# First value tiles in float32 from raw rows, and a new order at the head of a hybrid decoder step

## The chip, the cores and the metric

The kernel runs on one core of a Trainium2 chip. The metric is device time in microseconds (us) for one execution, the median of three runs. Five engines work side by side, each through its own queue in order: TensorE (PE, matmuls), VectorE (DVE), ScalarE (ACT), GpSimd (POOL) and SyncE (SP), whose queue issues the DMAs. Operands lie in SBUF, matmul results in PSUM, and inputs, outputs and scratch in HBM.

## The reference, cut to what matters

One inference step of a one-layer decoder, for a prompt of 2048 rows and for a decode batch of 64 rows (called the sample), with 1024 columns.

```python
h = rmsnorm(x, norm_w)                      # per row, then a weight for each column
z = h @ w_in                                # (2048 + 64) x 1024 by 1024 x 3600
q, k, v, qb, kb, vb, g_lr, gate_a, gate_b = jnp.split(z, split_points(), axis=-1)
q = rope(rmsnorm(heads(q, H_A), q_norm_w), pos)
k = rope(rmsnorm(heads(k, H_A), k_norm_w), pos)
o_a = attend(q, k, v)                       # three dilated windows, mixed by softmax weights
o_b, s_fin = gla_chunked(...)               # gated linear attention
y = x + (concat(o_a * silu(gate_a), rmsnorm(o_b) * silu(gate_b)) @ w_out)
```

The change touches the first 512 rows of the norm and of the products q, k and v.

## The kernel before, in words

The prompt is 16 tiles of 128 rows; the contraction over 1024 columns is 8 blocks (KT) of 128. Float32 accuracy comes from float16 pairs: rows and weights are each split into a high and a low part, and `project` adds three float16 products for each block (high by high, high by low, low by high), so one tile of one 512-wide output is 24 matmuls of 128x512 into a PSUM tile `acc_v_<tile>`, `acc_q_<tile>` and so on (pool `ps_Y`, two buffers).

Rows. `fetch` loads a tile of x. `squares` sums the squares of its rows (ScalarE, result `jk` thrown away), `rsqrt` makes the row factor `rs` on VectorE and ScalarE. For the first four tiles `prep_first` makes the high part on ScalarE and the low part on VectorE (`parts_of_rows`, tile `early_ht`), turns both by 16 float16 transposes on TensorE (`turned`, PSUM tiles `th_<tile>_<part>`), copies the turned high part by ScalarE and the low part by VectorE to `hl_<tile>`, and stores `hl` to `h_d` for later blocks. The sample's rows are normed (`x_s`), turned by 8 float32 transposes (`ptx`) and split to `hs`.

Weights. `fetch_w` loads 8 raw blocks of 128x512 (`wr_v`, `wr_q`, `wr_k`). `load_w` bounds them: for v, q and k VectorE takes the largest magnitude of each row of each block (`wm`), for the other blocks ScalarE sums squares (`jw`). `spread_max` takes the largest over the partitions by a transpose and a one-column matmul on TensorE (`mx`), with a VectorE reduction between the two. From it comes a power of two (`pw`), then the factors `ns`, and then each raw block gives a high part on ScalarE and a low part on VectorE (tile `w_v`, `w_q`, `w_k`).

Results. `post` handles a finished tile: for v ScalarE scales it to `vs` (stored as output) and makes `vp` (with VectorE's low part), which frees the PSUM tile. For q and k ScalarE makes the squares `sq` and the copy `zs`, then POOL and VectorE do the norm and the rotation, and ScalarE and VectorE write the parts `qp` or `kp`.

At the head (`first(0)`) v is computed for the sample and tiles 0 to 3, then q and k for tiles 0 to 3. After that come the other tiles with attention mixed in, the remaining projections, the linear attention and the output projection.

The order of each engine's queue is not the order of the code. `ORDER` lists, engine by engine, numbers of instructions in the order in which the code issued them; `in_order` binds the scheduler to that list. The lists come from a planner and are fixed for a kernel, so a change in what is issued comes with lists of its own for the whole kernel.

Of the kernel before, what the change touches and what calls it, by code (L numbers as in the profile page):

```python
# [18 lines left out]
P = 128  # L19
# [728 lines left out]
def tile_hymba(ctx: ExitStack, tc: tile.TileContext, A: dict):  # L748
# [276 lines left out]
    with ExitStack() as c1:  # L1025
# [153 lines left out]
        def prep_first(w_v):  # L1179
# [47 lines left out]
            for a in range(2):  # L1227
                turned(0, a)
# [1367 lines left out]
```

## Time and profile before

| | |
|---|---|
| runs | 1200.03, 1197.94, 1202.1 us; median 1200.03 |
| the profiled execution | 1201.56 us, its span on the core 1199.8 us |
| busy: TensorE / VectorE / ScalarE / POOL | 1162.0 / 919.0 / 785.1 / 542.2 us |
| TensorE idle, whole span | 37.8 us |
| TensorE busy in the first 40 us | 22.84 us |
| mean granted TensorE clock | 0.996 |
| moved by DMA | 283.13 MB, mean 236 GB/s |

A row of the instructions in order of time gives start and duration in us, engine, line, operation, output <- inputs, shapes and count; rows of equal instructions that follow each other are merged, and the bracket tells how long the engine was idle before it and what ended that. A row's duration of a matmul runs from its issue to the end of its way through the array, so that it overlaps the next one's.

### The profile page before, as it was taken

How to read it: one execution, taken by the hardware profiler on the slowest of the kernel's cores; microseconds unless marked ns; L12 is line 12 of the kernel's file. 1: busy time of each engine (PE TensorE's matmuls, PEld its weight loads, DVE VectorE, ACT ScalarE, POOL GpSimd, SP SyncE). 2: the span in 40 equal slices, each digit the busy share in tenths (PEclk: the TensorE clock that was granted, in tenths of full speed). 3: DMA queues.
4: the chain of work that ended last, by engine and by line, in shares of the span. 5: the costliest groups of instructions: out<-in, count | busy, mean ns of one | idle time of the engine just before them, and what ended most of it. 6: DMA issues, size and time to landing. Idle time of an engine off the chain costs nothing.

```text
span 1199.8 us, 27149 instructions
## 1 busy us (share of the span) xinstructions
PE 1162.0 (97%) x9542; PEld 714.5 (60%) x9542; DVE 919.0 (77%) x2489; ACT 785.1 (65%) x2152; POOL 542.2 (45%) x478
## 2 busy tenths in 40 slices
PE   4999999999999899999999999999999999999998
PEld 2544575566666566766777766646656566655543
DVE  7887888898989958878777755689788989743642
ACT  6645698778679968878767643777798764422220
POOL 0054444665548344662454558664534544311310
PEclk9999999999999999999999999999999999999999
DMA  8578967889768898799999977856672477999962
GB/s 292 196 188 203 252 186 145 228 216 233 165 196 227 199 254 282 245 279 273 281 267 256 278 225 212 256 181 232 205 258 85 137 263 263 320 392 398 375 216 79
DMA packets 235834, 283.13 MB, mean 236 GB/s; under 512 B 116193, under 2 KB 146866, under 8 KB 232626
## 3 DMA queue, kind: packets, MB, share of 16 engines
q1 hardware_dynamic: 235698, 281.40, 78.3%
q8 instruction: 75, 1.23, 0.4%
q14 instruction: 61, 0.50, 0.1%
HBM read 183.02 MB, written 75.24 MB: 215 GB/s over the span
## 4 chain that ended last, share of the span: by engine, by line
PE 81%; DVE 9%; ACT 3%; issue 3%; DMA 1%; POOL 1%; SPq 0%; POOLq 0%; DVEq 0%; ACTq 0%
PE Y L2181 12%; PE acc_q L1822 7%; PE acc_k L1822 7%; PE acc_qkb L1822 7%; PE acc_v L1822 6%; PE acc_vb L1822 6%; PE acc_g L1822 6%; PE t L1105 5%; PE s L1087 5%; PE acc_gb L1822 4%; PE O L1120 4%; PE OS L2438 2%; PE sc_e L932 1%; DVE p L1095 1%; PE tm L2146 1%
## 5 line engine op out<-in xcount | busy, mean ns | idle before, releaser
L1677 POOL TENSOR_TENSOR pr<-k,qb 128x512 f32<-128x512 f32 x128 | 168.8, 1319 | 126.6 <-DVE sck L1678 108.8
L1822 PEld LDWEIGHTS <-hr 128*128 128x128 f16 x1824 | 165.8, 98 | 86.9 <-issue 7.3
L1120 PE MATMUL O<-v,pt 128*128 128x64 f16 x1800 | 212.3, 193 | 3.6 <-POOL pt L1072 1.1
L1098 ACT ACTIVATE p<-p,st 128x256 f32<-128x256 f32 (+1 forms) x384 | 173.3, 454 | 36.0 <-DVE st L1095 35.0
L2181 PE MATMUL Y<-w_o,mh 128*128 128x512 f16 x768 | 187.4, 380 | 0.3 <-DVE xr L2188 0.3
L1120 PEld LDWEIGHTS <-pt 128*128 128x128 f16 x1800 | 145.5, 100 | 60.9 <-ACT pt L1064 2.7
L1822 PEld LDWEIGHTS <-hl 128*128 128x128 f16 x1248 | 116.8, 99 | 95.3 <-issue 1.8
L1072 POOL TENSOR_TENSOR pt<-p,pt 128x512 f16<-128x512 f32 (+1 forms) x80 | 95.6, 1195 | 151.4 <-DVE pt L1071 67.1
L1105 PE MATMUL t<-ident,p 128*128 128x128 f32 x600 | 147.5, 287 | 2.2 <-DVE pt L1065 1.2
L1822 PE MATMUL acc_g<-w_g,hr 128*128 128x272 f16 (+1 forms) x768 | 127.6, 276 | 0.9 <-ACT vbs L1460 0.9
L1087 PE MATMUL s<-kk,qq 128*128 128x256 f16 (+1 forms) x512 | 113.3, 265 | 1.2 <-DVE st L1095 0.9
L1822 PE MATMUL acc_v<-w_v,hl 128*128 128x512 f16 x384 | 113.5, 383 | 0.3 <-ACT hl L1195 0.3
L1822 PE MATMUL acc_vb<-w_vb,hr 128*128 128x512 f16 x384 | 113.3, 379 | 0.0
L1822 PE MATMUL acc_q<-w_q,hl 128*128 128x512 f16 x384 | 112.5, 379 | 0.0
L2181 PEld LDWEIGHTS <-mh 128*128 128x128 f16 x768 | 70.7, 98 | 68.5 <-issue 4.0
L1822 PE MATMUL acc_k<-w_k,hl 128*128 128x512 f16 x384 | 109.6, 379 | 0.2 <-DVE vp L1473 0.2
L1095 DVE CUSTOM_DVE_ANT_0 p<-s,m3w,scl_s 128x128 f32<-128x128 f32 (+1 forms) x256 | 92.7, 394 | 20.3 <-PE s L1087 9.0
L1678 DVE TENSOR_REDUCE sck<-pr 128x8 f32<-128x512 f32 x128 | 86.9, 679 | 23.5 <-POOL pr L1677 23.3
L1822 PE MATMUL acc_gb<-w_gb,hr 128*128 128x512 f16 x384 | 98.4, 380 | 0.8 <-DVE so_gb L1357 0.8
L1105 PEld LDWEIGHTS t<-ident,p 128*128 128x128 f32 x600 | 80.4, 141 | 24.8 <-ACT p L1098 3.8
L1822 PE MATMUL acc_qkb<-w_qkb,hr 128*128 128x512 f16 x288 | 85.9, 379 | 0.0
L1098 ACT ACTIVATION_READ_ACCUMULATOR p<-p,st 128x1 f32 x384 | 73.2, 191 | 0.0
(543 smaller groups left out, 2454.9 us busy)
## 6 DMA issues: line engine op xcount, KB each, us to landing
k<-in_cache_k_win SPq DMA_DIRECT2D x104, 256.0 KB
sv_b<-in_cache_v_win SPq DMA_DIRECT2D x24, 1024.0 KB
hr<-h_d SPq DMA_DIRECT2D x44, 512.0 KB
qb<-q_d SPq DMA_DIRECT2D x64, 256.0 KB
oc<-o_d SPq DMA_DIRECT2D x48, 264.0 KB
o_d<-o SPq DMA_DIRECT2D x64, 132.0 KB
x<-in_x_prompt SPq DMA_DIRECT2D x16, 512.0 KB
h_d<-hl SPq DMA_DIRECT2D x16, 512.0 KB
```

Of the source, the lines that this page charges most:

```text
L932: PE.matmul(sc[k0 : k0 + 64, o : o + 64], k[:, p * n + c * C + k0 : p * n + c * C + k0 + 64], qbd[:, :, p * (n // 2) + (c * C + k0) // 2 : ...
L1072: POOL.tensor_tensor(l, f, h, ALU.subtract)
L1087: PE.matmul(s_ps[:, i * w : (i + 1) * w], q, k, start=(n == 0), stop=(n == len(prods) - 1),)
L1095: DVE.tensor_tensor_reduce(s[:, sl], s_ps[:, sl], mask, neg, BIG, ALU.add, ALU.min, nmf(i))
L1098: ACT.activation(s[:, sl], s[:, sl], AF.Exp, bias=nmf(i), scale=-1.0, accum_out=denf(i))
L1105: PE.transpose(p_ps[:, i * P : (i + 1) * P], t["s"][:, i * P : (i + 1) * P], ident[:])
L1120: PE.matmul(o_, t["pt"][:, c, (i * nb + b) * P : (i * nb + b + 1) * P], vf(i, b)[:, d : d + HD], start=(b + n == 0), stop=(b == nb - 1 and ...
L1677: POOL.tensor_tensor(pr[:], kt, qt, ALU.mult)
L1678: DVE.tensor_reduce(out, pr[:].rearrange("p (u k d) -> p u k d", u=2, k=4), AX.X, ALU.add)
L1822: PE.matmul(z, a_[:, k, :], w[:, p_, k, cols], start=(k == 0 and i == 0), stop=(k == KT - 1 and i == 2),)
L2181: PE.matmul(Y[:], a_[:, k, :], w_[:, part, k, :512], start=(i == 0), stop=(i == len(prods) - 1),)
L2438: PE.matmul(OS[32 * x : 32 * x + 32, 0:256], ps(x), vs_[bb][:, 256 * u : 256 * u + 256], start=(i == 0), stop=(i == 13),)
```

## The change

1. `prep_first` multiplies tiles 0 and 1 by the raw weights of v in float32: raw rows `x` are turned by 8 float32 transposes for each tile (`xtp`), VectorE multiplies the turned rows by the norm weight while it takes them out of PSUM (`xt`, buffers `z4` and `z3`), and 8 float32 matmuls of 128x512 for each tile go straight to `acc_vx`. The row factor is applied when the result is taken out (`sc_v`, `exact_v`), so these two tiles of v need neither the split weights nor the split rows. They need both later, for q and k.
2. The row factors, parts and transposes come in the order tiles 2, 3, 0, 1. The sample's rows are loaded (`fetch("s")`, buffer `z3`, which tile 1's turned rows use first) and prepared behind all four tiles, and their product of v comes after the tiles'.
3. The bounds of w_q and w_k are made by sums of squares on ScalarE (`jw`), as those of the later weights are; w_v keeps the largest magnitudes.
4. Ten matmuls of a zero tile (`still` into `idle`) are issued ahead of all others.
5. The first DMAs are tile 0, the identity, one block of w_v, the norm weight, tile 1, the other blocks of w_v.

```diff
         def prep_first(w_v):
...
-            squares("s", ss[:NS, 0:1])
-            rsqrt(xp, rs[:NS, 0:1], ss[:NS, 0:1], 1.0 / D, NS, 1, "xs")
+            raws = fetched["v"]
+            zx = []
+            still = zp.tile([P, D], F16, name="still", tag="z1")
+            DVE.memset(still[:], 0.0)
+            idle = ps_O.tile([P, 512], F32, name="idle", tag="O")
+            for _ in range(10):
+                PE.matmul(idle[:], still[:, 0:P], still[:, 0:512], start=True, stop=True)
+            for t in range(2):
+                xt = zp.tile([P, KT, P], F32, name=f"xt_{t}", tag=("z4", "z3")[t], bufs=1)
+                for half in range(2):
...
+                    for i in range(4):
+                        k = 4 * half + i
+                        PE.transpose(pt[:, i], xs[t][:, k * P : (k + 1) * P], ident[:])
+                    DVE.tensor_tensor(
+                        xt[:, k4], pt[:], nw[:, k4].unsqueeze(2).to_broadcast([P, 4, P]), ALU.mult
+                    )
+                z = ps_Y.tile([P, 512], F32, name=f"acc_vx_{t}", tag="Y")
+                for k in range(KT):
+                    PE.matmul(z[:], xt[:, k], raws[k], start=(k == 0), stop=(k == KT - 1))
+                zx.append(z)
             squares(0, ss[:, 1:2])
             rsqrt(xp, rs[:, 1:2], ss[:, 1:2], 1.0 / D, P, 1, "x0", H_SCALE)
...
+            for t in range(2):
+                exact_v[t] = zx[t][:], sc[:, 0, t : t + 1], sc[:, 1, t : t + 1]
+            for t in (2, 3):
+                parts_of_rows(xs.pop(t), rs[:, t + 1 : t + 2], early_ht[:, t])
...
+            parts_of_rows(xs.pop(1), rs[:, 2:3], early_ht[:, 1])
+            for t in (2, 3, 0, 1):
+                for a in range(2):
+                    turned(t, a)
...
+            fetch("s")
+            squares("s", ss[:NS, 0:1])
...
-            exact = name in "vqk"
+            exact = name == "v"
...
-                ACT.activation(h, src, AF.Copy, scale=V_SCALE)
-                DVE.scalar_tensor_tensor(l, src, V_SCALE, h, ALU.mult, ALU.subtract)
+                by = exact_v[t][2] if t in exact_v else V_SCALE
+                ACT.activation(h, src, AF.Copy, scale=by)
+                DVE.scalar_tensor_tensor(l, src, by, h, ALU.mult, ALU.subtract)
...
-        fetch("s")
-        fetch_w("v", [0])
-        for t in (1, 2, 3):
+        fetch(0)
+        fetch_w("v", [1])
+        for t in (2, 3):
             fetch(t)
...
             for t in tiles:
+                if name == "v" and t in exact_v:
+                    z, by, _ = exact_v[t]
+                    post(name, z, by, P, t)
+                    yield
+                    continue
...
-                    for t in (["s"] if name == "v" else []) + tiles:
+                    for t in tiles + (["s"] if name == "v" else []):
```

`ORDER` is another list throughout; two of its lines:

```diff
-        "6-10 0 2 11 1 3-5 12-15 18 16 19-21 17 22-23 74 24-25 90-92 75 93 76 94-99 77 100-103 "
...
+        "0-7 10 14-17 11 8 12 26 13 30 27 31 28-29 32-33 18 34 19-23 42-43 35-41 44-45 24 46-48 "
...
```

TensorE's queue at the start of the program, before. `ptx` are the sample's transposes, `th` those of tile 0, `mx_v` the bound of w_v.

```order
L1219 MATMUL ptx_258<-ident,x_s 128x64 x4
L1189 LDWEIGHTS early_ht
L1189 MATMUL th_0_267<-ident_83,early_ht 128x128
L1257 MATMUL mx_v<-ident,w_v 1x128
L1219 MATMUL ptx_251<-ident,x_s 128x64
L1189 LDWEIGHTS early_ht
L1189 MATMUL th_0_267<-ident_83,early_ht 128x128
L1260 MATMUL mx_v<-mm_v,one_row 128x1
L1219 MATMUL ptx_251<-ident,x_s 128x64 x3
```

The same queue after, from the last of tile 1's float32 transposes (`xtp_..228` and `234`; those of tile 0, `206` and `212`, and eight of the zero matmuls stand ahead). `acc_vx_218` is tile 0's product, `acc_vx_240` tile 1's.

```order
L1217 MATMUL xtp_0_228<-ident,x_152 128x128 x2
L1217 MATMUL xtp_1_234<-ident,x_152 128x128 x2
L1223 MATMUL acc_vx_218<-wr_v_154,xt_205 128x512
L1223 MATMUL acc_vx_240<-wr_v_154,xt_227 128x512
L1223 MATMUL acc_vx_218<-wr_v_154,xt_205 128x512
L1223 MATMUL acc_vx_218<-wr_v_157,xt_205 128x512 x2
L1223 MATMUL acc_vx_218<-wr_v_161,xt_205 128x512 x2
L1292 MATMUL mx_v<-ident,w_v 1x128
L1295 MATMUL mx_v<-mm_v,one_row 128x1
L1223 MATMUL acc_vx_240<-wr_v_154,xt_227 128x512
```

Where the sample's and tile 0's transposes stood around the bound of w_v, there are now seven float32 products ahead of it, and nine behind it; all of tile 1's transposes stand ahead of the first product.

ScalarE's queue before, from the copy of the turned high part of tile 1 (`hl_191`) to the first parts of w_q.

```order
L1195 ACTIVATE hl_191<-th_0_319 128x1024
L1464 ACTIVATE vs_s<-za_446,wi_v 64x512
L1464 ACTIVATE vs_478<-acc_v_453,wi_v 128x512
L1472 ACTIVATE vp_481<-acc_v_453 128x8x64
L1195 ACTIVATE hl_192<-th_0_339 128x1024
L1195 ACTIVATE hl_193<-th_0_359 128x1024
L1338 ACTIVATE w_q<-wr_q_172,ns_q 128x512
L1338 ACTIVATE w_q<-wr_q_180,ns_q 128x512
```

The same queue after, from the fourth square of w_q's bound to the copy of the turned high part of tile 3 (`hl_191` is tile 3 here) and the root in w_q's bound.

```order
L1342 ACTIVATE jw_q_510,wm_q<-wr_q_176,nw 128x512
L1342 ACTIVATE jw_q_512,wm_q<-wr_q_178,nw 128x512
L1342 ACTIVATE jw_q_514,wm_q<-wr_q_180,nw 128x512
L1342 ACTIVATE jw_q_516,wm_q<-wr_q_182,nw 128x512
L1342 ACTIVATE jw_q_518,wm_q<-wr_q_184,nw 128x512
L1509 ACTIVATE vp_499<-acc_vx_240,sc_v 128x8x64
L1246 ACTIVATE early_ht<-x_152 128x1024
L1199 ACTIVATE hl_191<-th_0_350 128x1024
L1500 ACTIVATE vs_580<-acc_v_555,wi_v 128x512
L1355 ACTIVATE pw_q<-pw_q 128x1
L1273 ACTIVATE hs<-ptx_429 128x4x64
L1356 ACTIVATE pw_q<-pw_q 128x1
```

The squares of w_q, tile 1's `vp` and tile 0's high part now stand ahead of the copy that tile 3's product of v needs, and two more steps of the bound (`pw_q`) behind it.

More of the change, by code (lines that the diff above doesn't have):

```diff
@@ L1179, in prep_first @@
         def prep_first(w_v):
-            ss = xp.tile([P, 5], F32, name="ss_5", tag="ss5", bufs=1)
-            rs = xp.tile([P, 5], F32, name="rs_5", tag="rs5", bufs=1)
+            ss = xp.tile([P, 5], F32, name="ss_f", tag="ss5", bufs=1)
+            rs = xp.tile([P, 5], F32, name="rs_f", tag="rs5", bufs=1)
             hls = [hp.tile([P, 2, KT, P], F16, name=f"hl_{t}", tag="hl") for t in range(4)]
@@ L1195, in turned @@
                     ACT.activation(hls[t][:, a], pt[:], AF.Copy)
-            squares("s", ss[:NS, 0:1])
-            rsqrt(xp, rs[:NS, 0:1], ss[:NS, 0:1], 1.0 / D, NS, 1, "xs")
+            raws = fetched["v"]
[8 more added lines that the diff above has]
+                for half in range(2):
+                    pt = (ps_P, ps_S)[t].tile(
+                        [P, 4, P], F32, name=f"xtp_{t}_{half}", tag=("PT", "S")[t]
+                    )
+                    k4 = slice(4 * half, 4 * half + 4)
+                    for i in range(4):
[3 more added lines that the diff above has]
+                        xt[:, k4], pt[:], nw[:, k4].unsqueeze(2).to_broadcast([P, 4, P]), ALU.mult
+                    )
+                z = ps_Y.tile([P, 512], F32, name=f"acc_vx_{t}", tag="Y")
+                for k in range(KT):
+                    PE.matmul(z[:], xt[:, k], raws[k], start=(k == 0), stop=(k == KT - 1))
+                zx.append(z)
             squares(0, ss[:, 1:2])
@@ L1203, in prep_first @@
             squares(1, ss[:, 2:3])
+            squares(2, ss[:, 3:4])
+            squares(3, ss[:, 4:5])
+            rsqrt(xp, rs[:, 2:], ss[:, 2:], 1.0 / D, P, 3, "x3", H_SCALE)
+            next(w_v)
+            at_once(w_v)
+            sc = kp.tile([P, 2, 2], F32, name="sc_v")
+            DVE.tensor_scalar(sc[:, 0], rs[:, 1:3], 1.0 / H_SCALE, None, ALU.mult)
+            DVE.tensor_scalar(
+                sc[:, 1], rs[:, 1:3], inverse["v"][:], W_SCALE * V_SCALE, ALU.mult, ALU.mult
+            )
+            for t in range(2):
+                exact_v[t] = zx[t][:], sc[:, 0, t : t + 1], sc[:, 1, t : t + 1]
+            for t in (2, 3):
+                parts_of_rows(xs.pop(t), rs[:, t + 1 : t + 2], early_ht[:, t])
             x = xs.pop(0)
@@ L1207, in prep_first @@
             POOL.tensor_tensor(early_ht[:, 0, 1], x, early_ht[:, 0, 0], ALU.subtract)
+            parts_of_rows(xs.pop(1), rs[:, 2:3], early_ht[:, 1])
+            for t in (2, 3, 0, 1):
+                for a in range(2):
+                    turned(t, a)
+            for t in range(4):
+                hl = hls[t]
+                hT[t] = (hl[:, 0], hl[:, 1])
+                SP.dma_start(h_d[t * P : (t + 1) * P, :], hl[:].rearrange("p a k c -> p (a k c)"))
+            fetch("s")
+            squares("s", ss[:NS, 0:1])
+            rsqrt(xp, rs[:NS, 0:1], ss[:NS, 0:1], 1.0 / D, NS, 1, "xs")
             x = xs.pop("s")
             DVE.tensor_scalar(x[:NS], x[:NS], rs[:NS, 0:1], H_SCALE, ALU.mult, ALU.mult)
-            squares(2, ss[:, 3:4])
-            next(w_v)
             hs = hps.tile([P, KT, 2 * NS], F16, name="hs")
@@ L1225, in prep_first @@
                 DVE.tensor_tensor(hs[:, k4, NS:], ptv, hs[:, k4, 0:NS], ALU.subtract)
-            squares(3, ss[:, 4:5])
-            for a in range(2):
-                turned(0, a)
-            rsqrt(xp, rs[:, 2:], ss[:, 2:], 1.0 / D, P, 3, "x3", H_SCALE)
-            at_once(w_v)
-            for t in (1, 2, 3):
-                parts_of_rows(xs.pop(t), rs[:, t + 1 : t + 2], early_ht[:, t])
-            for t in (1, 2, 3):
-                for a in range(2):
-                    turned(t, a)
-            for t in range(4):
-                hl = hls[t]
-                hT[t] = (hl[:, 0], hl[:, 1])
-                SP.dma_start(h_d[t * P : (t + 1) * P, :], hl[:].rearrange("p a k c -> p (a k c)"))
             hT["s"] = hs
@@ L1261, in spread_max @@
             return pt[:, P : P + 1]
-        loaded, powers = {}, {}
+        loaded, powers, inverse, exact_v = {}, {}, {}, {}
         fetched = {}
@@ L1327, in load_w @@
             DVE.reciprocal(r[:], pw[:])
+            inverse[name] = r
             if rows:
@@ L1706, in tile_hymba @@
             POOL.memset(gmax[n_][:], 0.28)
-        fetch("s")
-        fetch_w("v", [0])
-        for t in (1, 2, 3):
+        fetch(0)
+        fetch_w("v", [1])
+        for t in (2, 3):
             fetch(t)
@@ L1845, in first @@
                 for name in "vqk":
-                    for t in (["s"] if name == "v" else []) + tiles:
+                    for t in tiles + (["s"] if name == "v" else []):
                         yield from project(name, [t])
                         if name == "v":
-                            if t == 0:
+                            if t == 1:
                                 at_once(load_w("q"))
```

1334 rows, old and new, of the table ORDER are left out of this document.

## The prediction

> **What bounds the kernel now.** I read the page's busy times first, then the busy times in stretches of 40 us, then TensorE's instructions in order of time over the first 75 us.
>
> ```profile
> span 1199.8 us, 27149 instructions
> PE 1162.0 (97%) x9542; PEld 714.5 (60%) x9542; DVE 919.0 (77%) x2489; ACT 785.1 (65%) x2152; POOL 542.2 (45%) x478
> ```
> ```profile
> 0.00:40.00 40.00, 22.84 (x136) 12.99 (x137) 30.32 (x74) 24.61 (x41) 2.45 (x6) 0.96 0.79 271
> 40.00:80.00 40.00, 40.00 (x187) 18.01 (x186) 34.39 (x77) 22.99 (x44) 15.25 (x17) 1.00 0.66 204
> ...
> 360.00:400.00 40.00, 36.50 (x386) 26.41 (x383) 37.52 (x113) 39.36 (x125) 30.38 (x23) 1.00 0.76 207
> ```
>
> In the second fence (stretch, its length, then busy us of PE, PE's weight loads, DVE, ACT, POOL, granted clock, DMA share, GB/s) TensorE is the bound: it idles 37.8 us in all, 17.2 of them before 40 us. From there on it is full but for some 20 us, short waits and the tail. So whatever lets it reach its dense stretch earlier counts one for one, and the head is where this change works.
>
> ```profile
> 17.70 1.46 PE L1822 MATMUL acc_v<-w_v,hl 128*128 128x512 f16 x3 [0.26 <-ACT hl L1195]
> 20.00 1.46 PE L1822 MATMUL acc_v<-w_v,hl 128*128 128x512 f16 x6
> 24.99 0.38 PE L1506 MATMUL acc_v_s<-w_v,hs 128*128 128x512 f16 x1 [2.34 <-DVE ra_x L818]
> 30.07 0.82 PE L1189 MATMUL th<-ident,early_ht 128*128 128x128 f16 x6 [1.61 <-DVE early_ht L1162]
> 35.02 0.50 PE L1189 MATMUL th<-ident,early_ht 128*128 128x128 f16 x6
> 50.75 0.81 PE L1822 MATMUL acc_q<-w_q,hl 128*128 128x512 f16 x3
> 53.55 17.37 PE L1822 MATMUL acc_q<-w_q,hl 128*128 128x512 f16 x79
> ```
>
> The head waits for normed rows and for weights, both made by VectorE and ScalarE. The last row prices a dense float16 matmul: (17.37-0.38)/78 = 0.218 us; a float16 transpose costs (0.50-0.22)/5 = 0.056. From 50.75 q runs, with 7 matmuls of v still mixed in (counted in the listing; 1.5 us). So v counts as finished at **52.3 us**. I compare this mark with the same mark after the change.
>
> **Float32 products for tiles 0 and 1.** They remove 48 float16 matmuls, 48 x 0.218 = 10.5 us, and add 16 float32 ones of 128x512. Before has none of that shape; the nearest is the decode state's update.
>
> ```profile
> L2080 PE MATMUL U_s<-vx,kdt_smp x16: 589/589/640, 740.8 to 791.4; 64*64 64x512 f32 x16
> 790.54 1.45 PE L2080 MATMUL U_s<-vx,kdt_smp 64*64 64x512 f32 x3
> ```
>
> The code issues 8 such matmuls, and the trace has 16 records: two each. Three records in 1.45 with a last one of 0.59 make 0.43 a record, so 0.86 a matmul and 13.8 us for 16. Bounds: 10.5 (float32 at three passes) to 27.5 (all of it at half clock); I take 13.8, since width and type agree. Sixteen float32 transposes add about 1.9 (0.12 each, from ptx below). TensorE thus does 5 us more, where it sat idle before.
>
> When can they run? Loads first.
>
> ```profile
> 4.33 1.06 ACT L1158 ACTIVATE jk_s<-x_s 64x1024 bf16<-64x1024 f32 x1 [2.32 <-DMA x_s<-in_x_sample]
> 6.92 0.69 DVE L1301 TENSOR_REDUCE wm_v<-wr_v 128x1 f32<-128x512 f32 x1 [0.23 <-DMA wr_v<-in_w_in]
> 11.35 0.66 PE L1219 MATMUL ptx<-ident,x_s 64*128 64x64 f32 x4 [11.35 <-DMA ident<-in_c_ident]
> 9.00:10.00 1.00, 0.00 (x0) 0.00 (x0) 0.97 (x4) 0.00 (x0) 0.00 (x0) 1.00 1.05 405
> ```
>
> At 6.92 us 1.05 MB had landed (sample rows, tile 0, one weight block). Now 1.38 MB (tile 0, identity, one weight block, tile 1) must land before tile 1 can be turned, and in the new listing tile 1's transposes stand ahead of the first float32 matmul: the other 0.33 MB at the 405 GB/s of the last row make it 7.7 us, and seven more weight blocks (1.83 MB) 12.3. Transposes and two evictions (0.65 each) put the first product at 8.8.
>
> After seven products (14.8) TensorE's queue holds the two instructions that spread the bound of w_v. They wait for VectorE: three evictions and eight row maxima.
>
> ```profile
> 8.25 1.26 DVE L1301 TENSOR_REDUCE wm_v<-wr_v 128x1 f32<-128x512 f32 x2
> 13.47 0.39 PE L1257 MATMUL mx_v<-ident,w_v 128*1 128x128 f32 x1
> 14.30 0.58 PE L1260 MATMUL mx_v<-mm_v,one_row 1*128 1x1 f32 x2
> 15.50 0.23 DVE L1329 TENSOR_SCALAR ns_v<-nw,pr_v 128x8 f32<-128x8 f32 x1
> 36.14 0.68 DVE L1473 SCALAR_TENSOR_TENSOR vp<-acc_v,vp 128x512 f16<-128x512 f32 x1
> ```
>
> From 8.6: two more evictions (0.6 each, the row at 36.14), eight maxima at 0.6, four small ones: 15.7. The round trip takes 1.1 (13.47 to 14.9, less at full clock), so TensorE goes on at 16.8, with all behind it held; the nine products left (7.7) and five transposes (0.3) end at **24.8**. The weights' scale is known 0.9 after that round trip, as before (14.9 to 15.73): 17.7, two us later than before.
>
> **What now orders the head: ScalarE.** From 17.7 on its queue is a chain without gaps up to the first q matmul. The prices:
>
> ```profile
> 16.62 1.02 ACT L1195 ACTIVATE hl<-th 128x1024 f16<-128x1024 f16 x1
> 17.54 3.16 ACT L1338 ACTIVATE w_v<-wr_v,ns_v 128x512 f16<-128x512 f32 x5
> 21.47 1.05 ACT L1158 ACTIVATE jk<-x 128x1024 bf16<-128x1024 f32 x1
> 25.81 3.23 ACT L1161 ACTIVATE early_ht<-x,rs 128x1024 f16<-128x1024 f32 x3 [1.12 <-DVE rs L820]
> 34.91 0.67 ACT L1464 ACTIVATE vs<-acc_v,wi_v 128x512 f32<-128x512 f32 x1
> 35.48 0.58 ACT L1472 ACTIVATE vp<-acc_v 128x512 f16<-128x512 f32 x1
> 363.78 0.71 ACT L1307 ACTIVATE jw_qkb<-wr_qkb,nw 128x512 bf16<-128x512 f32 x1
> 364.39 0.19 ACT L1307 ACTIVATION_READ_ACCUMULATOR jw_qkb<-wr_qkb,nw 128x1 f32 x1
> 364.49 0.71 ACT L1307 ACTIVATE jw_qkb<-wr_qkb,nw 128x512 bf16<-128x512 f32 x1
> ```
>
> Start to start (durations overlap by 0.1): weight part 0.61, square with its sum 0.71, rows' high part 1.05, copy of a turned tile 0.92, vs and vp 1.05 together. The new listing has between 17.7 and q: 16 weight parts (9.8), 8 squares of w_q (5.7), four rows' parts (4.2), three tile copies (2.8), three vs (1.7), three vp (1.4), the sample's square (1.0), eight small ones (1.4): 28.0, and 0.6 of waits: q's first matmul at **46.4**. TensorE has only about 16 us of work between 24.8 and there (48 x 0.218, 59 x 0.056, and 2.5 of the sample's transposes, its first products and w_q's bound), so it waits some 5 us, most of it for the copies of tiles 2 and 3, whose second one stands behind all eight squares (37.3). The bounds by squares thus move 16 x 0.6 = 9.6 us off VectorE, where some of them held the head, and put 11.4 us on the engine that now decides.
>
> At 46.4 four 0.218 and eight 0.11 matmuls of the sample's rows are left: v counts as finished at 48.15, a gain of 52.3-48.15 = 4.1.
>
> **Given back at w_k.** After q's first tile TensorE stands at 53.4 before the spread of w_k's bound. ScalarE needs vs, vp, eight squares, one copy and a small one after 46.4, 8.0 us: 54.4. TensorE waits 1.1. Its second instruction waits for a reduction queued on VectorE behind the first q tile's sums: 0.55. The two themselves take 0.6, which before fell ahead of 50.75. So 4.1-2.2 = **1.9 us** are left.
>
> ```profile
> 58.22 0.68 ACT L1383 ACTIVATE zs_q<-acc_q,wi_q 128x512 f32<-128x512 f32 x1
> 63.75 0.63 ACT L1497 ACTIVATE qp<-t_q 128x512 f16<-128x512 f32 x1 [2.94 <-DVE t_q L1419]
> ```
>
> The root in w_k's bound stands on ScalarE behind q's first finished tile, which comes 4.9 us after its zs (these two rows): zs ends at 55.6, so 60.5, then square and zs of tile 1 (63.1), the scale (64.2), eight casts and tile 2's square and zs (6.1): 70.5, low parts on VectorE to 74. k's first tile starts at 69.6, mixed with q's last, and asks for them in this order 1 or 2 us after each is there: I cost them at nothing. If that cover goes, k starts late by what they lack.
>
> **The rest.** Moving the sample's rows costs nothing by itself: their load waits until tile 1's products free the buffer (about 23) with one w_q block behind it on SP's queue, needed at 31. Zero matmuls run while nothing has landed: nothing, bounds -1.7 to +0.5. POOL loses nothing that is waited for. Every later instruction is the same, but the listing is another one, and its small waits fall elsewhere: zero.
>
> ```profile
> PE s L1087 <- DVE T_q L1536: 1.5, 1, 1.5
> ...
> PE sc_e L932 <- POOL kq_e L899: 0.2, 1, 0.2
> ```
>
> These are the first and the last of 22 rows of who kept TensorE waiting after 40 us; they add up to 15 us. Bounds of the new listing: -7.5 (half of them gone) and +7 (two more stretches like 360 to 400, 3.5 each).
>
> Sum: 1201.56 of the profiled execution less 1.9 is 1199.6; the median of the runs, 1200.03, lies 1.5 under that execution, so I forecast 1198.0.
>
> **The clock.** Three matmuls at 17.70 took as long as six at 20.00: half clock, 0.43 each, whatever the column of the granted clock says there (1.00). It fell again:
>
> ```profile
> 30.00:31.00 1.00, 0.93 (x7) 0.77 (x8) 1.00 (x3) 0.00 (x0) 0.00 (x0) 0.50 1.01 362
> 33.00:34.00 1.00, 1.00 (x11) 0.73 (x10) 0.10 (x1) 0.62 (x1) 0.00 (x0) 0.79 0.00 0
> ```
>
> The zeros (8 x 0.43 from 1.5 to 4.9) should have raised it by the first product, but TensorE then idles some 2 us until tile 1 lands, and it may fall. The Trainium skill ("TensorE: Matmul & The Clock Gate", Part 1) says that full speed comes after one busy window of about 3.4 us, and that the window runs freely of the kernel's start. The granted 0.50 from 30 to 33.4 agrees. By that rule the zeros can just miss a window, in which case the first products run at half clock for up to 3.4 us; the sum would then be 1198.7, since 1.0 of the 1.7 lost falls into the wait at mx_v.
>
> **Rivals.** (1) The listing helps later. The largest waits after 40 us are few and short, on ScalarE and VectorE; a listing that avoids half gives 1198-7.5 = 1190.5. For it: VectorE and ScalarE are full in those stretches only, and nothing structural is there; against: nothing in the change aims there. 0.30. (2) The other side: at 360 to 400 ScalarE is busy 39.36 of 40 us, and TensorE loses 3.5. If the new listing puts two further stretches of attention behind a full ScalarE, 7 us more: 1205. It decides from 1.9+3.6 = 5.5 us of added waits on. 0.18. (3) The clock falls under the products, and the float32 block is late by one or two windows (1.7 or 3.4, of which 1 is covered): 1198.7 to 1200.4, no gain to be seen. 0.08. (4) My forecast: 1198.0, own range 1195 to 1201.5. 0.44, of it 0.04 below 1196.4.
>
> **Numbers.** About 0.3%, 3.6 us, is what this measurement tells from no change. Faster 0.30+0.04 = 0.34, slower 0.18, the same 0.48. The range reaches to rivals 1 and 2: 1190.5 to 1205.
>
> **What would show it.** Right: products from about 9 to 25 us with 0.43 a record, a stop of 1 to 2 us before mx_v, ScalarE full from 18 to 54 us, q from about 46, a stop at mx_k near 54, idle before 40 us down from 17 to about 10. Wrong: q before 43 (ScalarE's chain is not the bound) or after 49, records of 0.86, or idle after 80 us that differs by over 4 us.

## The result, and the profile after

The change makes the kernel slower: 1207.59 us (median of 7 runs, 1203.97 to 1210.66) against 1200.24 us for the kernel before (7 runs beside them), a ratio of 1.0057 with an interval of 1.0037 to 1.0077. The forecast was 1198.0 us, its range 1190.5 to 1205. The profiled execution is the slowest of the seven, 1210.66 us with a span of 1208.9 us. The mean granted clock of the seven is 0.9953; that of the kernel before, in its 21 runs beside the first experiments, is 0.9975.

The page's span and first busy row, then the busy times in stretches (columns as in the prediction) of the kernel after:

```profile
span 1208.9 us, 27224 instructions
PE 1173.6 (97%) x9552; PEld 720.3 (60%) x9552; DVE 907.9 (75%) x2478; ACT 794.5 (66%) x2188; POOL 554.3 (46%) x478
```
```profile
0.00:40.00 40.00, 32.45 (x129) 16.09 (x130) 23.75 (x66) 28.05 (x57) 2.17 (x5) 0.96 0.70 234
40.00:80.00 40.00, 38.62 (x205) 18.23 (x204) 31.50 (x71) 30.58 (x64) 11.43 (x16) 1.00 0.69 222
...
800.00:840.00 40.00, 35.41 (x329) 20.94 (x328) 33.54 (x80) 30.43 (x76) 18.55 (x22) 0.96 0.60 182
840.00:880.00 40.00, 37.70 (x255) 23.73 (x255) 32.16 (x96) 28.14 (x73) 19.96 (x19) 0.96 0.62 205
```

The same two late stretches of the kernel before:

```profile
800.00:840.00 40.00, 37.88 (x372) 23.58 (x370) 36.92 (x109) 33.05 (x83) 19.42 (x22) 1.00 0.69 223
840.00:880.00 40.00, 39.93 (x279) 23.70 (x277) 32.29 (x85) 31.49 (x77) 20.73 (x19) 1.00 0.70 223
```

In the first 40 us TensorE's idle time falls from 17.2 to 7.6 us. That is not 9.6 us won: its busy time there grows from 22.84 to 32.45 because it has more to do, the matmuls of zeros (3.6 us, the row at 1.45 us further below) and the float32 products and transposes (some 5 us more by the prediction's sum). From 800 to 880 us, in the linear attention, it does 4.7 us less than before in the same time, and the clock is at 0.96. That place is some 720 us behind anything that the change rewrites.

A second reading says the same. I take the start of each matmul in the trace after, subtract that of the same matmul before, and take the median for each 20 us of the kernel before (from 60 us on the two traces hold the same matmuls):

```
from us        60   120   280   660   780   800   820   840   860   940   960  1160
after, us    -0.6  -0.5  -1.4  +3.4  +2.1  +5.1  +6.4  +8.9  +9.7 +11.5  +7.5  +9.2
```

At 120 us the kernel is 0.5 us ahead; from 780 to 860 us it loses 7.6 us. From 280 to 660 us it loses 4.8 us as well, and two stretches at half clock of 3.41 us each lie there in this execution (from 391.1 and 554.9 us, 1.7 us lost each time). (The fall at 955 us is the profiled run of before, which lost 3.4 us of clock there.)

### The profile page after: what moved, and what is told of

Same layout as the page of the kernel before. It is cut to its first block, busy times and chain, and to the rows that moved or that the text cites. A ratio compares the mean times of both kernels' runs of the same rounds, so it can differ in the third digit from the quotient of the medians.

```text
span 1208.9 us, 27224 instructions
## 1 busy us (share of the span) xinstructions
PE 1173.6 (97%) x9552; PEld 720.3 (60%) x9552; DVE 907.9 (75%) x2478; ACT 794.5 (66%) x2188; POOL 554.3 (46%) x478
## 4 chain that ended last, share of the span: by engine, by line
PE 79%; DVE 9%; ACT 5%; DMA 3%; issue 3%; POOL 1%; SPq 0%; POOLq 0%; DVEq 0%; ACTq 0%
PE Y L2223 13%; PE acc_qkb L1864 7%; PE acc_k L1864 6%; PE acc_vb L1864 5%; PE acc_g L1864 5%; PE acc_q L1864 5%; PE t L1109 5%; PE acc_gb L1864 5%; PE s L1091 5%; PE acc_v L1864 4%; PE O L1124 4%; PE OS L2480 2%; PE sc_e L936 1%; PE acc_vx L1223 1%; PE tm L2188 1%
## 5 line engine op out<-in xcount | busy, mean ns | idle before, releaser
L1124 PE MATMUL O<-v,pt 128*128 128x64 f16 x1800 | 217.1, 194 | 2.4 <-ACT p L1102 0.8
L2223 PE MATMUL Y<-w_o,mh 128*128 128x512 f16 x768 | 190.2, 379 | 1.2 <-DVE xr L2230 1.2
L1124 PEld LDWEIGHTS <-pt 128*128 128x128 f16 x1800 | 149.0, 101 | 65.0 <-issue 5.7
L1864 PEld LDWEIGHTS <-hl 128*128 128x128 f16 x1200 | 110.5, 99 | 87.8 <-issue 2.6
L1864 PE MATMUL acc_g<-w_g,hr 128*128 128x256 f16 (+1 forms) x768 | 127.2, 277 | 0.8 <-DVE za L1557 0.8
L1864 PE MATMUL acc_k<-w_k,hl 128*128 128x512 f16 x384 | 112.1, 379 | 0.1
L1715 DVE TENSOR_REDUCE sck<-pr 128x8 f32<-128x512 f32 x128 | 87.0, 680 | 25.5 <-POOL pr L1714 25.2
L1864 PE MATMUL acc_v<-w_v,hl 128*128 128x512 f16 x336 | 103.2, 379 | 3.0 <-DVE vp L1510 1.5
L1864 PE MATMUL acc_gb<-w_gb,hr 128*128 128x512 f16 x384 | 101.1, 387 | 2.2 <-DVE so_gb L1393 2.1
L1109 PEld LDWEIGHTS t<-ident,p 128*128 128x128 f32 x600 | 81.0, 142 | 25.2 <-ACT p L1102 5.5
L2265 POOL TENSOR_TENSOR oc<-oc 128x512 f32<-128x512 f32 x32 | 41.8, 1322 | 73.3 <-DVE oc L2258 68.5
```

The lines of the kernel that those rows point to most:

```text
L1109: PE.transpose(p_ps[:, i * P : (i + 1) * P], t["s"][:, i * P : (i + 1) * P], ident[:])
L1124: PE.matmul(o_, t["pt"][:, c, (i * nb + b) * P : (i * nb + b + 1) * P], vf(i, b)[:, d : d + HD], start=(b + n == 0), stop=(b == nb - 1 and ...
L1715: DVE.tensor_reduce(out, pr[:].rearrange("p (u k d) -> p u k d", u=2, k=4), AX.X, ALU.add)
L1864: PE.matmul(z, a_[:, k, :], w[:, p_, k, cols], start=(k == 0 and i == 0), stop=(k == KT - 1 and i == 2),)
L2223: PE.matmul(Y[:], a_[:, k, :], w_[:, part, k, :512], start=(i == 0), stop=(i == len(prods) - 1),)
L2265: eng.tensor_tensor(o_[g], o_[g], w[:, g].unsqueeze(2).to_broadcast([P, NH, HD]), ALU.mult)
```

## What the two stops are

Who kept TensorE waiting from 780 to 870 us (total, times, longest; rows of 0.4 us and more; first the kernel after, then before):

```profile
PE sc_e L936 <- issue: 2.4, 1, 2.4
PE acc_gb L1864 <- DVE so_gb L1393: 2.1, 1, 2.1
PE O L2030 <- DVE kq_e L907: 1.0, 1, 1.0
PE U L2022 <- DVE Sbd L2043: 0.9, 1, 0.9
```
```profile
PE sc_e L932 <- DVE mn L2208: 0.9, 1, 0.9
PE acc_gb L1822 <- DVE so_gb L1357: 0.8, 1, 0.8
PE U L1980 <- DVE Sbd L2001: 0.4, 1, 0.4
```

The first stop, in order of time (start, duration, engine, line, operation):

```profile
799.18 1.26 POOL L837 TENSOR_TENSOR prod_e<-zqk_e 128x512 f32<-128x512 f32 x1
799.61 2.67 DVE L818 TENSOR_SCALAR rv_o_smp<-oss_smp 64x4 f32<-64x4 f32 x1
800.41 0.62 POOL L903 TENSOR_TENSOR kq_e<-kq_e,sums_e 128x256 f32<-128x256 f32 x1
801.00 1.26 POOL L1714 TENSOR_TENSOR pr<-k,qb 128x512 f32<-128x512 f32 x1
802.31 0.20 ACT L819 ACTIVATE rr_o_smp<-rv_o_smp 64x4 f32<-64x4 f32 x1 [3.41 <-DVE rv_o_smp L818]
802.42 0.40 ACT L895 ACTIVATE qbd<-kq_e 64x256 f32<-64x256 f32 x1
802.73 0.71 ACT L1397 ACTIVATE sa_gb<-sa_gb,ones 128x512 f32<-128x512 f32 x1
803.46 0.41 ACT L895 ACTIVATE qbd<-kq_e 64x256 f32<-64x256 f32 x1
803.97 0.64 PE L936 MATMUL sc_e<-qbd,kq_e 128*64 128x64 f32 x8 [2.39 <-issue]
```

`sc_e` needs the second `qbd`, and `qbd` needs the `kq_e` that POOL ended at 801.03. ScalarE stood idle then, but its next instruction was `rr_o_smp`, a logarithm on 64x4 numbers for the sample's output, and that waited for VectorE's `rv_o_smp`, which ended at 802.28 only. So TensorE waited for a result that it doesn't need, because a queue is served in order. In the kernel before's list both `qbd` stand ahead of `rr_o_smp`; here are ScalarE's rows from a run below (experiment 3) with that list:

```profile
796.58 0.40 ACT L866 ACTIVATE qbd<-kq_e 64x256 f32<-64x256 f32 x1
...
798.50 0.21 ACT L790 ACTIVATE rr_o_smp<-rv_o_smp 64x4 f32<-64x4 f32 x1 [0.99 <-DVE rv_o_smp L789]
```

The second stop is on VectorE. The gate's next product `acc_gb` needs the PSUM tile that `so_gb` takes out:

```profile
838.13 1.25 DVE L907 TENSOR_TENSOR kq_e<-kq_e,sums_e 128x256 f32<-128x256 f32 x1
839.31 0.33 DVE L2043 SCALAR_TENSOR_TENSOR Sbd<-Sbd,sums_e,U 64x128 f32<-64x128 f32 x1
839.56 0.99 DVE L913 TENSOR_TENSOR sums_e<-sums_e 128x32 f32<-128x32 f32 x1
840.48 0.74 DVE L1393 TENSOR_SCALAR so_gb<-acc_gb,wi_gb 128x512 f32<-128x512 f32 x1
841.14 0.41 DVE L907 TENSOR_TENSOR kq_e<-kq_e,sums_e 128x256 f32<-128x256 f32 x1
```

Three operations stand ahead of `so_gb`, and one of them, the same form as the row at 841.14, takes 1.25 us instead of 0.41. Soon after the end of each stop the trace has a stretch of 3.41 us in which half the clock is granted (from 804.1 and from 841.6 us, 0.1 and 0.4 us after the stops), 1.7 us lost each time.

**Theory L:** the loss is in the lists behind the head, at such places. **Rival H:** the changed head costs it, by something that shows late. A third: chance of the clock.

## Experiments

Each run stands beside runs of the kernel before on the same chip; the ratio is against those. The lists of `ORDER` are cut by the start times in a trace: what an engine has started by then keeps one kernel's order, what is left follows the other's.

**1 and 2. Head and lists apart.**

```diff
 the changed kernel (1)                     the kernel before (2)
 ORDER to 75 us: its own                    ORDER to 75 us: its own
-from 75 us: its own                       -from 75 us: its own
+from 75 us: the kernel before's           +from 75 us: the changed kernel's
```

> The changed kernel with its own lists of instructions up to 75 us (all that the change rewrites), and from there the kernel before's lists, instruction for instruction. Theory L (the lists after the head cost the time): about 1200 us, within 2 us of the kernel before, since the two reach k's last product 0.2 us apart; no jump of the lag between 790 and 850 us. Rival H (the changed head costs it, through clock, buffers or transfers that show late): 1205 to 1208 us, as the changed kernel.

> The kernel before, unchanged in what it computes and how, with its own lists up to 75 us and from there the changed kernel's lists. Theory L: 1205 to 1208 us, with a lag that jumps by 5 to 10 us between 790 and 850 us. Rival H: 1200 us.

The second is clear: 1208.42 us, ratio 1.0065 (1.0046 to 1.0084). The kernel before, with none of the change, is as slow as the changed one when it runs by the new lists, and its waits from 780 to 870 us are those of the changed kernel to 0.1 us; its lag goes from -0.5 us at 780 to +7.1 at 860 us:

```profile
PE sc_e L907 <- issue: 2.4, 1, 2.4
PE acc_gb L1797 <- DVE so_gb L1332: 2.1, 1, 2.1
```

The first missed: 1206.15 us, ratio 1.0042 (1.0029 to 1.0055), where L had 1200. But the loss is in another place. Its lag goes from -1.0 at 60 us to +4.6 at 80 us and never jumps at 800; from 68 to 92 us the trace has

```profile
PE acc_k L1834 <- ACT zs_k L1389: 4.3, 2, 3.2
```

The kernel before's lists put the last query tile's chain of small operations (VectorE and ScalarE by turns) ahead of the eviction `zs_k`; in the changed head that chain is later, so k's accumulator is not freed (run 8 tries this). The head and its list have to fit each other.

**3 and 4. Which part of the lists.**

```diff
 the changed kernel (3)                     the changed kernel (4)
 ORDER to 780 us: its own                   ORDER to 75 us: its own
-from 780 us: its own                      -75 to 780 us: its own
+from 780 us: the kernel before's          +75 to 780 us: the kernel before's
                                            from 780 us: its own
```

> The changed kernel with its own lists up to 780 us, and the kernel before's from there. Theory L, with the loss between 790 and 850 us as the lag of the matmuls shows it: 1200 to 1202 us. If the lists lose their time before 780 us, or after it only because of what they carried over: 1205 to 1208 us.

> The changed kernel with its own lists up to 75 us, the kernel before's from 75 to 780 us, and its own again behind that. Theory L with the loss behind 780 us: 1205 to 1208 us, with the jump of the lag between 790 and 850 us. If the place is not there: about 1200 us. A third theory, that no place carries the loss and it is the clock that fell at chance places in the profiled run: this and the three others lie between 1200 and 1207 us without the pattern.

1201.2 us, ratio 1.0003 (0.9992 to 1.0015), and 1213.74 us, ratio 1.0102 (1.0083 to 1.0121). The four runs add up: lists from 780 us on cost 6.4 us (1207.6 against 1201.2) or 7.6 (1213.74 against 1206.15); the other list from 75 us on costs 5 us under the new head. The third kernel, the whole change with its own lists to 780 us, is level with the kernel before.

**5, 6, 7. The two places by themselves.** One instruction moved in a list each, then both:

```diff
 ScalarE, 802 us (5)
-rr_o_smp  qbd  sa_gb  qbd
+qbd  sa_gb  qbd  rr_o_smp
 VectorE, 838 us (6)
-so_gb(3)  kq_e  Sbd  sums_e  so_gb(4)
+so_gb(3)  so_gb(4)  kq_e  Sbd  sums_e
```

> The changed kernel with one instruction of ScalarE's list moved: the logarithm rr_o_smp, which waits at 799.7 to 802.3 us for VectorE's stretched rv_o_smp, goes behind the two copies to qbd that TensorE's sc_e is waiting for. Theory L, by waits in order on ScalarE and VectorE: the stop at sc_e falls from 2.4 to about 1 us, and the clock's half speed that follows at 804 us stays away (1.7 us): 3.1 us less than the changed kernel, about 1204.5 us. If the late lists lose in many small places: 1207 us.

> The changed kernel with one instruction of VectorE's list moved: the eviction so_gb (840.5 us), for whose accumulator the gate's product acc_gb stands still for 2.1 us, goes ahead of the products kq_e, the update of Sbd and sums_e that stand before it, to 838.2 us. Theory L: the stop of 2.1 us goes, and the half speed at 841.6 us with it (1.7 us): 3 to 3.8 us less than the changed kernel, about 1204 us; if kq_e is late instead, because it now stands behind the eviction, nothing is won: 1207 us.

> Both moves together. Theory L: the two add up, 1207.6 less 3.1 and 3.4, about 1201 us, level with the kernel before, and no half speed between 790 and 850 us. If each move only hands its wait to the next place: 1204 us or more.

1205.55 (ratio 1.0033, 1.0021 to 1.0045), 1205.9 (1.0041, 1.0025 to 1.0056) and 1203.43 us (1.0025, 1.0015 to 1.0034): by the medians 2.0, 1.7 and 4.2 us less than the changed kernel, half to two thirds of what I expected. Only the last is clear of noise: its interval lies below the changed kernel's (1.0037 to 1.0077), those of 5 and 6 overlap it. So it is shown that the two moves together bring time back, by the medians 4.2 of the 6.4 us; how much each brings, and that they add up, is only likely. With both moved the trace has from 780 to 870 us

```profile
PE U L1993 <- DVE Sbd L2014: 1.7, 2, 0.9
PE acc_gb L1835 <- DVE so_gb L1364: 1.2, 1, 1.2
PE O L2001 <- DVE kq_e L878: 1.0, 1, 1.0
PE O L2001 <- ACT ob_c L950: 0.8, 1, 0.8
PE sc_e L891 <- issue: 0.3, 1, 0.3
```

`sc_e` fell from 2.4 to 0.3 although `rv_o_smp` took 2.67 us again, so the move did it. (In run 6's trace it fell to 0.7 without this move, since `rv_o_smp` took only 0.94 us there: the first stop isn't the same in every execution.) But another eviction `so_gb` now waits 1.2, and small stops behind `Sbd` and `ob_c` make up the rest. No half clock is left between 790 and 870 us, and the mean granted clock of these three kernels' runs is 0.9975 to 0.9979, that of the kernel before.

**8. Is the seam all of run 1's loss?** As run 1, cut at 110 us instead of 75.

```diff
-from 75 us: the kernel before's
+from 110 us: the kernel before's
```

> The changed kernel with its own lists up to 110 us and the kernel before's from there. The same with the cut at 75 us took 1206 us, with stops of 3.2 and 1.1 us at acc_k behind ScalarE's zs_k at 84 and 92 us, since the kernel before's lists put the last query tile's chain of small operations ahead of zs_k. If that is all of it, the stops go and this takes 1200 to 1201.5 us. If the changed head costs time under any list but its own: 1204 us or more.

1202.55 us, ratio 1.0011 (0.9999 to 1.0023): a microsecond above what I expected, below the bound I had set for the other case. Its waits behind `zs_k` are gone; the lag is +0.1 at 120 us, in a run in which half the clock fell under the first products (from 8.8 us).

**9, 10, 11. Parts of the change, on the third kernel's lists (1201.2 us).**

```diff
-for _ in range(10): PE.matmul(idle[:], ...)        # 9, with still and its memset
-exact = name == "v"
+exact = name in "vk"                               # 10
+exact = name in "vqk"                              # 11
```

In 10 and 11 the nine operations of a bound stand ahead of `w1_k`, and at four places from 31 us to `w1_q`, in VectorE's list.

> The changed kernel with its own lists to 780 us and the kernel before's behind (1201.2 us), without the ten matmuls on zeros. They run from 1.5 to 5.0 us, while TensorE has nothing else until tile 1 lands at 8.7 us. If they only fill idle time: no difference, 1200 to 1202.5 us. If they hold the granted clock up for the first products: the half speed comes at about 9 us or a second one comes before 40 us, and the time is 1.7 us more, about 1203 us.

> The same base (1201.2 us), with the bound of w_k taken from maxima on VectorE again (nine operations of about 0.6 us, placed ahead of w1_k near 52 us, where VectorE is idle for 3 us) instead of squares on ScalarE (eight of about 0.7 us from 48 to 56 us). If k's bound is covered in either form, since w_k's power is asked for at 56 us and k's first product comes only at 70 us: 1200.5 to 1202 us. If the squares hold the evictions behind them up: about 1 us less.

> As the run of k's bound alone, and the bound of w_q from maxima on VectorE too, between 31 and 39 us. By the prediction's account ScalarE's chain sets q's first matmul (28 us of work behind 17.7 us), and the squares of w_q are 5.2 us of it: ScalarE would be through 5 us earlier, but VectorE has only some 4 us free there, so w1_q comes at 38 to 39 us instead of 36.5 us and q's first matmul 1 to 2 us later: 1202 to 1203.5 us. If ScalarE is what binds: q's first matmul at 46 us or earlier and 1199.5 us.

Without the zeros 1202.14 us, ratio 1.0016 (1.0003 to 1.0029): 0.9 us above the third kernel, which these runs can't tell from none, nor from the 1.7 us of the other case. The traces show that the zeros do more than fill idle time. Without them the float32 products begin at half clock:

```profile
10.29 7.75 PE L1189 MATMUL acc_vx<-wr_v,xt 128*128 128x512 f32 x14
```

In the third kernel, with the zeros, the same 14 records take 6.28 us, and q's first matmul comes at 48.39 instead of 49.84. But the clock can fall all the same: half of it is granted from 8.8 us in the kernel after, and a later half clock is there with the zeros (from 29.6 in the third kernel) and without (from 30.5). With k's maxima 1200.26 us, 1.0007 (0.9994 to 1.002): covered in either form, although TensorE's `mx_k` now waits 1.6 us. With q's maxima too 1209.23 us, 1.0072 (1.0053 to 1.0091), far above the 1202 to 1203.5 I expected. q's first matmul comes 7.3 us later than in the third kernel (48.39). Of these, 3.0 us were there before the maxima began: the first float16 product of v comes at 30.82 instead of 27.78 us, behind a later landing of tile 1 and 6.83 us at half clock from 8.0 us on. The rest comes with the maxima:

```profile
42.16 0.37 PE L1262 MATMUL mx_q<-ident,w_q 128*1 128x128 f32 x1 [2.44 <-DVE w_q L1319]
...
55.65 4.26 PE L1834 MATMUL acc_q<-w_q,hl 128*128 128x512 f16 x19 [1.17 <-DVE scl_q L1761]
```
```profile
30.00:40.00 10.00, 6.20 (x39) 3.06 (x39) 9.63 (x22) 5.18 (x9) 2.57 (x1) 1.00 0.57 195
40.00:50.00 10.00, 7.84 (x43) 3.98 (x44) 7.32 (x20) 4.57 (x8) 0.00 (x0) 0.83 0.44 143
```

ScalarE (fourth busy time) is half idle there, and VectorE is full from 30 to 40 us; TensorE waits for it 1.6 us for the sample's rows (to 38.1 us) and 2.4 us for the bound of w_q (the row at 42.16). So VectorE has no room there for this bound, and the squares on ScalarE make it. Much of the loss in time is clock: half of it is granted again from 42.1 us, and the mean over its runs is 0.9925 against 0.9969 in the third kernel, by which I estimate 5 of the 8 us; that the one at 42.1 us follows from the longer stop is likely but wasn't tried.

**12, 13, 14. Does the head leave anything?** The changed kernel with its own lists to 300 us, where its lead is largest; then two moves near 710 us (the load goes ahead of six other transfers, not of eight as the expectation has it) that take away the stops at which this lead was lost; then those moves in the kernel before.

```diff
-from 780 us: the kernel before's
+from 300 us: the kernel before's                        # 12
 SyncE, 709 us (13 and 14)
-zqk_smp  k  ga_d  qb  k  zg_d  ga_d  zqk_e
+zqk_smp  zqk_e  k  ga_d  qb  k  zg_d  ga_d
 ScalarE, 722 us (13 and 14)
-qbd  vbs
+vbs  qbd
```

> The changed kernel with its own lists up to 300 us and the kernel before's from there: in the run with the cut at 780 us the lead over the kernel before was 1.3 us at 80 us and 2.2 us at 280 us, and was lost again by 0.9 to 1.2 us each near 340 and 660 us, while the kernel before's lists from 110 us on held what they were given to within 0.2 us. Theory L (the lists decide, the head leaves a lead of 1 to 2 us): 1198.5 to 1200 us, a little faster than the kernel before. If the lead is no more than chance of the clock: 1201 us or more.

> The changed kernel with its own lists to 300 us and the kernel before's behind, and two moves near 710 us: SyncE's load of zqk_e goes ahead of eight other transfers, directly behind that of zqk_smp (issued near 706 us instead of 709.2 us), and ScalarE's eviction vbs ahead of the copy to qbd that waits 4.6 us for VectorE. If the lead is lost at these two stops: it is held past 725 us, and the time falls by 2 to 2.7 us, to 1197 to 1197.7 us, below the kernel before. If the lead ends for another reason (the stops come again a little later): 1199.5 us.

> The kernel before with the same two moves. Its stops there are 0.9 us each: if they are all that is won, 1.8 us less than the kernel before, about 1199 us, and 1.5 to 2 us above the first run, which is then the head's lead. If it takes as little as the first run, there is no lead.

1199.64 us, ratio 1.0001 (0.9988 to 1.0014); 1200.94 us, 1.0004 (0.9991 to 1.0018); 1201.27 us, 1.0007 (0.9998 to 1.0017). None can be told from the kernel before. The trace of the twelfth holds a lead of 2.2 us from 300 to 660 us and has 0.2 left at 720. Its stops there, from 690 to 800 us, and those of the thirteenth:

```profile
PE acc_g L1835 <- ACT vbs L1467: 1.5, 1, 1.5
PE ptg_e L830 <- DMA zqk_e<-zqk_d: 1.2, 1, 1.2
```
```profile
PE acc_g L1835 <- DVE so_g L1364: 1.2, 1, 1.2
PE acc_vb L1835 <- DVE so_g L1364: 1.1, 1, 1.1
PE ptg_e L830 <- DVE la_smp L851: 0.3, 1, 0.3
```

The two stops went, and two others of 2.3 us came, behind VectorE's `so_g`. What I expected of the thirteenth fell; so did the fourteenth's 1.8 us, where a stop of 1.4 us behind `so_g` and one of 0.3 came in place of the two. I found no version that beats both kernels.

## Why the prediction was wrong, point by point

**The failed step: "its small waits fall elsewhere: zero".** This term of the sum, the new listing, costs 6.4 us behind 780 us (1207.6 against 1201.2 in run 3), near the upper bound I gave it (+7). Run 2 shows that by itself, with none of the change; run 7 shows that two places make most of it. Rival 2 had the kind (two more places, 3.5 us each) and nearly the time, 1205, but not the place: I looked to attention behind a full ScalarE, and it was the linear attention, where from 800 to 840 us neither is full (ScalarE is busy 30.43 and VectorE 33.54 of 40 us) and single instructions stand in the wrong order. I gave it 0.18. I knew that every list of the kernel was new and had no way to price that but the waits before; the chance of a loss should have been as large as that of a gain.

**TensorE's head.** In the order that I told, and up to 2 us late. The kernel after:

```profile
1.45 3.59 PE L1207 MATMUL idle<-still 128*128 128x512 f16 x8 [1.45 <-DVE still L1204]
8.74 2.17 PE L1217 MATMUL xtp<-ident,x 128*128 128x128 f32 x9 [2.49 <-DMA x<-in_x_prompt]
10.70 6.92 PE L1223 MATMUL acc_vx<-wr_v,xt 128*128 128x512 f32 x14
18.41 6.28 PE L1223 MATMUL acc_vx<-wr_v,xt 128*128 128x512 f32 x14
29.20 0.38 PE L1864 MATMUL acc_v<-w_v,hl 128*128 128x512 f16 x1 [1.52 <-DVE vp L1510]
49.24 4.26 PE L1864 MATMUL acc_q<-w_q,hl 128*128 128x512 f16 x19 [1.17 <-DVE scl_q L1791]
56.36 0.27 PE L1292 MATMUL mx_k<-ident,w_k 128*1 128x128 f32 x1
```

The float32 price holds: two records each, (6.28-0.6)/13 = 0.44 a record. Tile 1 landed at 8.7, not 7.7; the first product came at 10.7, not 8.8; the block ended about 26.6, not 24.8. About half of that is the load and half the clock, which fell under the transposes (2.17 us for nine, 1.20 in run 3). In run 3, where it didn't, these marks are 8.2, 9.4 and 25.2. Either way the stop before `mx_v` was 0.4 us (before its second instruction; in run 3 as much again before its first), where I had 1 to 2.

**The gain at q.** Forecast 46.4 for q's first matmul, measured 49.24 (48.39 in run 3). The first of ScalarE's weight parts and its last `vp` before q:

```profile
19.36 0.72 ACT L1374 ACTIVATE w_v<-wr_v,ns_v 128x512 f16<-128x512 f32 x1 [2.14 <-DVE ns_v L1365]
47.88 0.59 ACT L1509 ACTIVATE vp<-acc_v 128x512 f16<-128x512 f32 x1
```

From the one to the end of the other ScalarE is busy nearly throughout, and it takes 29.1 us (29.7 in run 3) where I had 28.7: that account holds. But it began 1.7 us late (0.2 in run 3), and behind it VectorE's own part of `vp` and the small `scl_q` take another 0.8 us, which I had left out. TensorE's other waits on VectorE (`vp` 1.5, the sample's `rv_xs` 0.8 before the row at 30.85 us) fall into the 5 us that it waits in my sum. That ScalarE alone is short of time doesn't hold: run 11 shows that VectorE has no room for q's bound either. With the sample's products still to come (1.75 us, the prediction's) v counts as finished at 51.0 (50.1 in run 3), a gain of 1.3 (2.2), not 4.1.

**Given back at w_k.** No stop came at `mx_k`: the sample's products fill the time to 56.36. Only the instructions themselves remain of the 2.2 us. So two errors nearly cancelled: the lead on the kernel before's trace is 1.3 us at 80 to 120 us in run 3, where 1.9 was forecast, and 0.5 in the changed kernel's own profiled run.

**That a lead at the head counts one for one.** Not shown, and not borne out: the lead of 2.2 us in run 12 is lost at 680 to 725 us, where the kernel before has stops of 1.8 us that a late kernel doesn't have (run 1's lag falls from 4.8 to 2.6 there). The time of 1199.64 us is no different from before's.

**The clock.** Rival 3 had half the clock under the first products. Of the twelve profiled runs that have the changed head and the zeros, seven have it from 7.9 to 9.8 us (the changed kernel from 8.8), two from 29 to 30 us and three not before 40. A stretch of 3.41 us costs 1.7 us. What I left out was the clock behind later stops. At the two late places four profiled runs (after, 2, 4 and, at the second place, 5) have seven stops of 2.1 to 2.4 us: five were followed within 1.1 us by 3.41 us at half clock, two were not. The Trainium skill ("TensorE: Matmul & The Clock Gate", the section on why this matters) sets the limit for gaps at about 3 us; here the measurement decides: stops of 2.1 us were mostly followed by it, stops of 0.9 to 1.5 us near 391 and 554 us were in four profiled runs (after, 7, 8, 9), and run 1's stop of 3.2 us at 84 us was not. So the length of a stop alone doesn't tell. By the mean granted clocks, 0.9953 against 0.9969 in run 3, I estimate that some 1.9 of the 6.4 us are clock and the rest the waits. By the same estimate the clock makes 2.6 to 3.1 us of what runs 5 to 7 bring back (0.9975 to 0.9979): in run 7 that is most of its 4.2 us, so the moves may have paid through the clock more than through the stops themselves. (The estimate is rough: the changed kernel's executions have means from 0.992 to 0.998.)

**What stays open.** The 2.2 us that remain with both moves are read from the waits, not tested one by one. That the half clock follows from the stop before it is read from the order in time and from its absence in run 7's trace; what decides when it follows and when not, no run shows.

## What to carry over

When a change comes with new lists for the whole kernel, give the lists an experiment of their own: the old code under the new order, or the new code under the old order beyond the part that changed. Here the order cost more than the change could bring. In such an order look for a small operation whose input comes late standing ahead of the copy or eviction that TensorE waits for; but expect the next wait to take over a third to a half of what a move frees (runs 5 to 7), or all of it (13 and 14).

## What the runs showed of the hardware

`rv_o_smp`, an operation on 64x4 numbers, took 0.94, 2.02 or 2.67 us by run, and ended each time about 0.1 us or less after the end of a POOL operation: after one of them (0.94, runs 5 and 6) or after three in a row (2.02 before, where the first was nearly over, and 2.67 after: 799.18, 800.41 and 801.00 above). The Trainium skill ("SBUF — State Buffer", the section on two separate sides) says that VectorE and GpSimd share one pair of ports as an exclusive lock: a GpSimd operation takes it, and so does a VectorE operation in a mode of two ports or with two inputs from SBUF (against a GpSimd operation that reads SBUF), and whichever starts first holds it for the whole instruction while the other stands still. The durations agree with that, and add that a VectorE instruction can stand still for several of POOL's running one behind the other; that `rv_o_smp` runs in such a mode, and that the lock is the cause, no run here shows by itself. By its durations a small operation on VectorE is an uncertain thing to queue others behind.
